# A decoder layer with two linear-attention mixers: two chunks in one matmul in the delta rule's inverse, with a wider step table

## The chip, the cores and the metric

The kernel runs on one core of one Trainium2 chip. The metric is the device time of one execution in microseconds (us). Three runs of the kernel before gave 2825.11, 2827.06 and 2832.34 us; the median is 2827.06.

## The reference

One layer of a decoder: 2048 tokens of width 1024, float32. An input projection feeds four heads of a gated delta rule and four heads of HGRN2 (128 wide each); then come an output projection, an MLP of 4096 with squared ReLU, and a gated embedding. The part that the change touches is the delta rule, in chunks of c tokens:

```python
lmat = jnp.einsum('bhncd,bhnsd->bhncs', k_beta, k) * decay
a_mat = jnp.eye(c) + jnp.where(strict, lmat, 0.0)
u = solve(v_beta)                                  # a_mat u = v_beta
w = solve(k_beta * jnp.exp(gc)[..., None])
...
def step(s, inp):
    v_new = u_n - w_n @ s
    o = qg_n @ s + qk_n @ v_new
    s = s * cd_n[..., None, None] + kt_n.T @ v_new
    return s, o
```

So each chunk needs the inverse of a unit triangular matrix, and the chunks of one head follow each other through the state `s`. The kernel uses chunks of 128 tokens.

## The kernel before

Everything is one function, `trunk`, for one core. Tokens are cut into four quarters (`q`) of 512 (`QT`), each into four chunks (`NC`) of 128. The first half of the execution is the mixer stage, the second the output projection, MLP and gate, which the change leaves alone.

**The mixer stage.** A list of projections (`works`) is gone through in order: per quarter one small one for the decays (`ab`) and eight for each of four heads (k, q, v, z of the delta rule, then f, i, q, g of HGRN2). Each is 24 matmuls of 128x512 on split float32 operands. After every eight of them `tick()` is called: this text calls what happens there a *turn*. A projection has three turns, a head 24. In a turn, Python generators that stand in an agenda take their next step; between two `yield`s lies one step. `gdn_mixer` (delta rule) and `hgrn_mixer` are such generators, with one step for each entry of the tables `A_STEPS` and `B_STEPS`, counted in turns from the head's start; the last head has tables of its own, `A_LAST` and `B_LAST`. A step at 34 is thus taken at turn 10 of the next head, beside that head's own steps; in one turn the older head comes first, and in a head the delta rule ahead of HGRN2. TensorE's order and that of SP's DMA queue are the program's; the other engines' order is the scheduler's.

**The delta rule's steps.** The convolution (`conv_silu`) leaves k, q, v as tiles of 128x512 (`kT`, `qT`, `vT`) with Silu as one ACT instruction. Then, by step (in turns of the head):

- 3 and 6: the decays are loaded and spread (`gf`), the masked exponentials `e` are made from the mask `negm`.
- 7 to 9: k is turned on TensorE (bank `psk`); its squared norm gives `rk`, `cc`, `ncc`, `inv` (through a power on POOL).
- 10: eight matmuls into two banks (`kk`), from which DVE makes the chunk's triangular matrix `u` and the scores `qk`, and multiplies `kT` and `qT` by `gf`.
- 12: v is turned; the 32x32 diagonal blocks of `u` are stored to memory (`ud`, four DMAs).
- 14 to 22: the blocks come back spread over the partitions (`sys`), and DVE inverts them all by a triangular solve of 16 passes (L621 to L626).
- 24 and 26: the inverses go out (`xd`) and come back as block diagonals into `xx`, which POOL cleared (one 128x512 memset, four DMAs).
- 28: DVE transposes them (four instructions, L641).
- 30 to 36: two levels (`lev` 5 and 6) fill in the blocks off the diagonal: 4 matmuls `psp` (L651), a copy `half`, then 8 or 4 matmuls `psd` (L657, L658) and copies back into `xx` (L662, L663). All have 64 columns, one matmul for each chunk and side.
- 38 to 49: the recurrence over the four chunks, three steps each: `psa` (kg and the state, then DVE makes `r`, L671), `psb` (the inverse and `r`, then ACT makes `w`, L676), `psc` (then DVE makes the new state, L681) with two matmuls into `pso`. One turn lies between two steps.
- 50 to 59: `finish` squares, sums over the partitions (`nrm`, L261), stores the row (L266), loads it as `m` (L269), takes a power on POOL, stores that (L274), loads it spread (L236), scales and stores (L530).

Banks: `pp` has four, for nearly all of these; `po` has two, for `pso`; `pm` two, for the projections. `kT` and `qT` have two buffers, `ktail`, `vt` and `qk` two, `xx`, `um` and `half` one.

Of the kernel before, what the change touches and what calls it, by code (L numbers as in the profile page):

```python
# [20 lines left out]
P = 128  # L21
# [20 lines left out]

C_IDENT, C_NEG, C_UNIT, C_MASK = 0, 1, 2, 3
N_CONST = C_MASK + len(LEVELS)
# [17 lines left out]
def constants():  # L62
    j = np.arange(P)[:, None]
    i = np.arange(P)[None, :]
    c = np.zeros((P, N_CONST, P), np.float32)
    c[:, C_IDENT] = (i == j)
    c[:, C_NEG] = np.where(j <= i, 0.0, -1e30)
    c[:, C_UNIT] = (i % SB == GC * (j % GR) + i // SB)
# [11 lines left out]
def trunk(ctx, tc, x, xT, pT, vecs, w_in, w_ab, gdn_a_log, gdn_dt_bias, w_out, w_up, w_down,  # L80
# [19 lines left out]
    def blk(c):  # L100
        return slice(c * P, (c + 1) * P)
# [6 lines left out]
    ident = cst[:, C_IDENT, :]  # L108
    negm = cst[:, C_NEG, :]
# [3 lines left out]
    def over_chunks(m):  # L113
        return m[:, None, :].broadcast_to([P, NC, P])

# [281 lines left out]
    with mixers as mctx:  # L397
# [11 lines left out]
        V.memset(bound, 0.0)  # L409
        um = {lev: mp.tile([P, NC, P], F32, name=f"um{lev}") for lev in (5, 6)}  # L410
        half = mp.tile([P, NC, P], F32, name="half")
        for t in (*um.values(), half):
            V.memset(t, 0.0)
# [40 lines left out]
        def decays(ps, q):  # L454
# [18 lines left out]
            nc.sync.dma_start(gd, gb[0:4, :])  # L473
            yield
            ps = bank(f"ps_gb_{q}", ph)
            for c in range(NC):
                PE.transpose(ps[:, c * 36 : (c + 1) * 36], gb[:, blk(c)], ident[:36, :36])
            gcol = sm.tile([P, NC, 36], F32, tag="gcol", name=f"gcol_{q}", bufs=2)
# [12 lines left out]

        def conv_silu(ps, j, name, tag, bufs):

# [7 lines left out]
            y = m2.tile([P, QT], F32, tag=tag, name=f"y_{name}", bufs=bufs)  # L501
            call(clock[0], lambda: S.activation(y, acc, AF.Silu))
            return y

        def turned(src, name, pool=None):
# [10 lines left out]
        def finish(q, h, pso, zt, extra, eps, n):  # L516
# [13 lines left out]
            nc.sync.dma_start(mixd[q][h], og)  # L530

        def gdn_mixer(q, h, live):

# [14 lines left out]
            e = mt(f"e_{n}", "e")  # L548
            V.tensor_tensor(e, gf, over_chunks(negm), ALU.add)
            for c in range(NC):  # L550
# [32 lines left out]
            for c in range(0, NC, 2):  # L583
                ps = bank(f"kk_{n}_{c}", pp).rearrange("p (a b i) -> p a b i", a=2, b=2)
                for a in range(2):
                    sl = blk(c + a)
                    PE.matmul(ps[:, a, 0, :], kT[:, sl], kT[:, sl], start=True, stop=True)
                    PE.matmul(ps[:, a, 1, :], kT[:, sl], qT[:, sl], start=True, stop=True)
                for a in range(2):
                    V.scalar_tensor_tensor(u[:, c + a, :], ps[:, a, 0, :], ncc[:, c + a : c + a + 1],  # L590
                                           e[:, c + a, :], ALU.mult, ALU.mult)
                V.tensor_tensor(qk[:, c : c + 2, :], ps[:, :, 1, :], e[:, c : c + 2, :], ALU.mult)
            V.tensor_tensor(kT, kT, flat(gf), ALU.mult)
            V.tensor_tensor(qT, qT, flat(gf), ALU.mult)
# [10 lines left out]
            yield  # L605
            for lev in (5, 6):
                s = LEVELS[lev]
                for o in range(0, P, 2 * s):
                    S.activation(um[lev][o : o + s, :, o + s : o + 2 * s], u[o : o + s, :, o + s : o + 2 * s], AF.Copy)
            sys = mt(f"sys_{n}", "sys", 1, (P, SB, SB))  # L610
# [22 lines left out]

            xx = mt(f"xx_{n}", "xx", 1, (P, NC, 2 * P))
            G.memset(xx[:, :, P:], 0.0)
            for b in range(NB):
                nc.sync.dma_start(xx[b * SB : (b + 1) * SB, :, P + b * SB : P + (b + 1) * SB],
                                  xd[:, b].rearrange("c j i -> j c i"))
            yield
            for c in range(NC):  # L640
                V.transpose(xx[:, c, :P], xx[:, c, P:])  # L641
            for lev in (5, 6):
                s = LEVELS[lev]
                yield

                psp = bank(f"psp_{n}_{lev}", pp)[:, : QT // 2].rearrange("p (c b s) -> p c b s", c=NC, s=s)
                left = xx[:, :, :P].rearrange("p c (b two s) -> p c b two s", two=2, s=s)[:, :, :, 0]
                right = xx[:, :, P:].rearrange("p c (b two s) -> p c b two s", two=2, s=s)[:, :, :, 1]
                part = half.rearrange("p c (b two s) -> p c b two s", two=2, s=s)[:, :, :, 0]
                for c in range(NC):  # L650
                    PE.matmul(psp[:, c], um[lev][:, c, :], left[:, c], start=True, stop=True)  # L651
                S.activation(part, psp, AF.Copy)
                yield
                psd = bank(f"psd_{n}_{lev}", pp).rearrange("p (c two b s) -> p c two b s", c=NC, two=2, s=s)
                for c in range(NC):
                    if lev == 5:
                        PE.matmul(psd[:, c, 0], xx[:, c, P:], part[:, c], start=True, stop=True)  # L657
                    PE.matmul(psd[:, c, 1], half[:, c, :], right[:, c], start=True, stop=True)  # L658
                for i in range(P // (2 * s)):
                    o = 2 * s * i  # L660
                    if lev == 5:
                        S.activation(left[o + s : o + 2 * s, :, i], psd[o + s : o + 2 * s, :, 0, i], AF.Copy)  # L662
                    S.activation(right[o : o + s, :, i], psd[o : o + s, :, 1, i], AF.Copy)  # L663
            yield
            pso = bank(f"pso_{n}", po)
            for c in range(NC):
# [6 lines left out]
                psb = bank(f"psb_{n}_{c}", pp)[:, :P]  # L673
                PE.matmul(psb, xx[:, c, P:], r, start=True, stop=True)
                w = m2.tile([P, P], F32, tag="w", name=f"w_{n}_{c}")
# [117 lines left out]
        def to_k(ps, q, h, g, b):  # L793
            g["k"] = conv_silu(ps, 4 + h, f"kg{q}_{h}", "kT", 2)

        def to_q(ps, q, h, g, b):
            g["q"] = conv_silu(ps, h, f"qg{q}_{h}", "qT", 2)

        def to_v(ps, q, h, g, b):
            g["v"] = conv_silu(ps, 8 + h, f"vg{q}_{h}", "vT", 1)  # L800

# [873 lines left out]
```

## Time and profile before

| | us |
|---|---|
| median of three runs | 2827.06 |
| lowest, highest | 2825.11, 2832.34 |
| the profiled execution | 2829.28 |
| its span in the profile | 2827.5 |
| TensorE (PE) busy | 2736.0 |
| VectorE (DVE) busy | 2041.8 |
| ScalarE (ACT) busy | 1448.3 |
| TensorE's granted clock | 0.991 of full |

The profile lists instructions by engine, line and tile. In a group's row stand its form (partitions x elements), its count, then the busy time and the mean in ns of one, then the idle time of the engine just before and what ended it. PE is TensorE's matmuls, PEld its weight loads, SPq the DMA queue of SyncE. An f32 matmul of the mixers appears as two instructions. In the views of waits a row says who waited for whom: us in total, times, longest. A busy TensorE may still be slower than it could be, since a matmul's end is modelled and the next one starts before it.

### The profile page before, as it was taken

Reading aid. Unit: us, or ns where it says so; the run is one execution under the profiler, and the core shown is the slowest. Engines: PE = TensorE matmul, PEld = TensorE weight load, DVE = VectorE, ACT = ScalarE, POOL = GpSimd, SP = SyncE. Lnnn points to the kernel's source line nnn. Section 1 sums busy time; section 2 is a strip of 40 time slices with the busy share of each in tenths; the row PEclk is TensorE's granted clock in tenths of the full one; section 3 lists DMA queues with packets and bytes.
Section 4 is the critical chain, followed back from the end, with each engine's and each line's share of the span. In section 5 each row is a group of like instructions: output and inputs, shape, how many; then the busy total and the mean of one; then the engine's idle time right before and its main releaser. Section 6 shows DMA issues by size and latency. Waiting matters only on the chain.

```text
span 2827.5 us, 38753 instructions
## 1 busy us (share of the span) xinstructions
PE 2736.0 (97%) x13041; PEld 2258.5 (80%) x13041; DVE 2041.8 (72%) x4236; ACT 1448.3 (51%) x2761; POOL 110.3 (4%) x104
## 2 busy tenths in 40 slices
PE   7999999999999999898999999999999999999999
PEld 5788788888888888786778887888888888887887
DVE  6677767786777777667797876767787765567775
ACT  6565545454545444565555555555555445455431
POOL 0000000000000000000000000000100000001000
PEclk9999999999999999999999999999999999999999
DMA  7766667656656665686575547666454446577663
GB/s 246 262 219 214 210 228 256 208 199 227 226 198 210 219 210 174 201 294 228 176 241 191 199 145 241 209 212 242 152 199 159 148 148 218 190 253 243 206 217 116
DMA packets 268598, 589.19 MB, mean 208 GB/s; under 512 B 55642, under 2 KB 59960, under 8 KB 249200
## 3 DMA queue, kind: packets, MB, share of 16 engines
q1 hardware_dynamic: 268400, 586.72, 61.9%
q8 instruction: 103, 1.69, 0.2%
q14 instruction: 95, 0.78, 0.1%
HBM read 419.68 MB, written 166.92 MB: 207 GB/s over the span
## 4 chain that ended last, share of the span: by engine, by line
PE 48%; DMA 4%; DVE 3%; ACT 2%; issue 2%; SPq 0%; POOL 0%; DVEq 0%; ACTq 0%; POOLq 0%
PE u L1031 21%; PE d L1031 18%; PE mmg L1031 6%; PE mmo L1031 2%; DMA raw_out<-in_w_out_dram 1%; DMA da<-sumd 1%; DMA db<-hid 1%; DMA b<-h1d 0%; DVE w_out L162 0%; DMA mixT<-mixd 0%; DVE t L162 0%; ACT w_out L161 0%; ACT L1068 0%; DVE b L1178 0%; PE mmo L991 0%
## 5 line engine op out<-in xcount | busy, mean ns | idle before, releaser
L963 PE MATMUL mm<-xt,w 128*128 128x512 f32 x3072 | 781.2, 402 | 4.9 <-DVE acc_vg L499 4.5
L963 PEld LDWEIGHTS mm<-xt,w 128*128 128x128 f32 x3072 | 562.3, 190 | 117.9 <-issue 3.4
L1031 PE MATMUL d<-db,da 128*128 128x512 f32 x2688 | 612.6, 389 | 4.0 <-DVE db L215 3.5
L1031 PE MATMUL u<-t,wu 128*128 128x512 f32 x2604 | 608.0, 396 | 3.4 <-ACT wu L161 3.3
L1031 PEld LDWEIGHTS d<-db,da 128*128 128x128 f32 x2688 | 504.1, 188 | 111.8 <-DVE db L215 5.7
L1031 PEld LDWEIGHTS u<-t,wu 128*128 128x128 f32 x2604 | 489.5, 188 | 121.2 <-ACT wu L161 4.1
L215 DVE TENSOR_TENSOR db<-db 128x512 fp32r<-128x512 f32 x224 | 161.5, 721 | 73.9 <-ACT db L214 73.5
L1360 DVE TENSOR_TENSOR u<-u,u 128x512 f32<-128x512 f32 x224 | 150.3, 682 | 74.4 <-PE u L1031 74.1
L1031 PE MATMUL mmo<-mixT,w_out 128*128 128x512 f32 x720 | 171.7, 399 | 11.4 <-DVE w_out L162 7.8
L214 ACT ACTIVATE db<-db 128x512 fp32r<-128x512 f32 x224 | 140.8, 629 | 81.0 <-DMA db<-hid 80.0
L1031 PE MATMUL mmg<-h2T,wg 128*128 128x512 f32 x768 | 178.1, 394 | 0.0
L1401 ACT ACTIVATE u<-u 128x512 f32<-128x512 f32 x128 | 80.9, 632 | 181.4 <-DVE u L1360 181.0
L1031 PEld LDWEIGHTS mmo<-mixT,w_out 128*128 128x128 f32 x720 | 136.8, 191 | 45.3 <-DVE w_out L162 9.1
L1031 PEld LDWEIGHTS mmg<-h2T,wg 128*128 128x128 f32 x768 | 144.3, 188 | 33.5
L162 DVE TENSOR_TENSOR da<-da 128x512 fp32r<-128x512 f32 x128 | 92.9, 726 | 89.4 <-ACT da L161 89.1
L161 ACT ACTIVATE da<-da 128x512 fp32r<-128x512 f32 x128 | 80.5, 629 | 137.3 <-DMA da<-sumd 120.2
L621 DVE TENSOR_TENSOR pr_g<-xs_g,sys_g 128x16 f32<-128x16 f32 (+14 forms) x240 | 94.2, 392 | 5.1
L161 ACT ACTIVATE wu<-a 128x512 fp32r<-128x512 f32 x124 | 74.1, 624 | 46.1 <-DMA a<-in_w_up_dram 43.9
L225 POOL TENSOR_TENSOR acc_y<-acc_y,sq_y 128x512 f32<-128x512 f32 x28 | 38.7, 1384 | 1396.6 <-ACT sq_y L224 1396.6
L162 DVE TENSOR_TENSOR wu<-a,wu 128x512 fp32r<-128x512 f32 x124 | 84.7, 686 | 3.8 <-ACT wu L161 3.8
L1402 ACT ACTIVATE u<-u 128x512 f32<-128x512 f32 x128 | 80.8, 631 | 3.7
L162 DVE TENSOR_TENSOR da<-dr,da 128x512 fp32r<-128x512 f32 x96 | 66.2, 689 | 16.5 <-ACT da L161 14.4
(362 smaller groups left out, 3892.3 us busy)
## 6 DMA issues: line engine op xcount, KB each, us to landing
w<-cache_in SPq DMA_DIRECT2D x96, 1024.0 KB
db<-hid SPq DMA_DIRECT2D x224, 256.0 KB
cache_in<-w SPq DMA_DIRECT2D x32, 1024.0 KB
hid<-u SPq DMA_DIRECT2D x128, 256.0 KB
da<-sumd SPq DMA_DIRECT2D x128, 256.0 KB
a<-in_w_up_dram SPq DMA_DIRECT2D x124, 256.0 KB
hid<-ht SPq DMA_DIRECT2D x96, 256.0 KB
dr<-in_w_down_dram SPq DMA_DIRECT2D x96, 256.0 KB
```

Source lines behind the costliest of these rows:

```text
L161: S.activation(t[:, 0], raw, AF.Copy)
L162: eng.tensor_tensor(t[:, 1], raw, t[:, 0], ALU.subtract)
L214: S.activation(t[:, 0], plain(t), AF.Copy)
L215: V.tensor_tensor(t[:, 1], plain(t), t[:, 0], ALU.subtract)
L225: eng.tensor_tensor(acc, acc, sq, ALU.add)
L621: V.tensor_tensor(pr[:, :, :, 0:i], xs[:, None, :, 0:i].broadcast_to([P, 2, GC, i]), sys[:, 0:i, i : i + 2].rearrange("p j two -> p two j" ...
L963: PE.matmul(ps, *terms[i], start=i == 0, stop=i == nt - 1)
L1031: PE.matmul(ps, a, b, start=start, stop=stop)
L1360: V.tensor_tensor(c[new], c[old], ps, ALU.add)
L1401: S.activation(c[k], c[k], AF.Relu)
L1402: S.activation(c[k], c[k], AF.Square)
```

## The change

*Two chunks in one matmul.* The four 32-blocks of every odd chunk are kept in reverse order, so that its triangular matrix has its blocks on the other side of the diagonal; an even and an odd chunk then fill one 128x128 matrix. The reversal is made where the data arise: Silu of k and v is written in two halves, the odd one with blocks backwards; the decays are transposed from a reversed copy (`back`); a second mask plane is added; `u` of odd chunks is made with `e` read backwards; `kT` is multiplied by `gf` in two halves. q stays as it is. The inverse works on pairs: `xt` (block diagonals of both chunks of a pair), `xn` (its transpose, one DVE instruction), `um` and `part` by pair, ten matmuls of 128 columns instead of twenty of 64, and a last set of copies into `xt_full`, from which `psb` reads.

*The step table.* The steps from 30 on move: psp5 to 32, the inverse to 32 to 38, the recurrence to 40 to 55 with two turns between `psa` and `psb`, `finish` to 56 to 65. `A_LAST` is given the same values as before from its sixteenth entry on.

*Buffers.* `kT` and `qT` get three.

```diff
-A_STEPS = ((3, 6, 7, 8, 9, 10, 12, 14, 16, 17, 18, 19, 20, 21, 22, 24, 26, 28, 30, 32, 34, 36)
-           + tuple(range(38, 50)) + (50, 52, 54, 55, 57, 59))
+A_STEPS = ((3, 6, 7, 8, 9, 10, 12, 14, 16, 17, 18, 19, 20, 21, 22, 24, 26, 28, 32, 34, 36, 38)
+           + (40, 42, 43, 44, 46, 47, 48, 50, 51, 52, 54, 55)
+           + (56, 58, 60, 61, 63, 65))
...
-            call(clock[0], lambda: S.activation(y, acc, AF.Silu))
+            def last():
+                if back:
+                    S.activation(even(y), even(acc), AF.Silu)
+                    S.activation(odd(y), odd_back(acc), AF.Silu)
+                else:
+                    S.activation(y, acc, AF.Silu)
+            call(clock[0], last)
...
-            V.tensor_tensor(kT, kT, flat(gf), ALU.mult)
+            V.tensor_tensor(even(kT), even(kT), even(flat(gf)), ALU.mult)
+            V.tensor_tensor(odd(kT), odd(kT), odd_back(flat(gf)), ALU.mult)
...
-            for lev in (5, 6):
-                s = LEVELS[lev]
-                for o in range(0, P, 2 * s):
-                    S.activation(um[lev][o : o + s, :, o + s : o + 2 * s], u[o : o + s, :, o + s : o + 2 * s], AF.Copy)
+            up = by_pair(u)
+            for g in range(NB):
+                S.activation(um[5][rows_of(g), :, rows_of(g ^ 1)], up[rows_of(g), :, g % 2, rows_of(g ^ 1)], AF.Copy)
+            for a in range(2):
+                S.activation(um[6][halves[a], :, halves[1 - a]], up[halves[a], :, a, halves[1 - a]], AF.Copy)
...
-            xx = mt(f"xx_{n}", "xx", 1, (P, NC, 2 * P))
-            G.memset(xx[:, :, P:], 0.0)
...
-            for c in range(NC):
-                V.transpose(xx[:, c, :P], xx[:, c, P:])
...
+            xt = mt(f"xt_{n}", "xt", 1, (P, NC, P // 2))
+            xn = mt(f"xn_{n}", "xn", 1, (P, NC, P // 2))
+            G.memset(xt, 0.0)
+            for g in range(NB):
+                nc.sync.dma_start(xt[rows_of(g), :, rows_of(g % 2)], xd[:, g].rearrange("c j i -> j c i"))
+            yield
+            V.transpose(flat(xn), flat(xt))
+            yield
+            def pairs(out, lhsT, rhs):
+                for p in range(2):
+                    PE.matmul(out[:, p], lhsT[:, p], rhs[:, p], start=True, stop=True)
...
+            psp = pair_bank("psp5")
+            pairs(psp, um[5], two(xn))
+            for g in range(NB):
+                S.activation(part[5][rows_of(g), :, rows_of(g ^ 1)], psp[rows_of(g), :, rows_of(0 if g % 2 else 3)],
+                             AF.Copy)
+            yield
+            psx, pst = pair_bank("psx5"), pair_bank("pst5")
+            pairs(psx, two(xt), part[5])
+            pairs(pst, part[5], two(xt))
+            for g, to in ((1, 0), (2, 1)):
+                V.tensor_copy(by_pair(xn)[rows_of(g), :, g // 2, rows_of(to)], psx[rows_of(g), :, rows_of(3 * to)])
+            for g in range(NB):
+                at_b = rows_of(1 + g % 2)
+                S.activation(two(xt)[rows_of(g), :, at_b], pst[rows_of(g), :, at_b], AF.Copy)
+            yield
+            psp = pair_bank("psp6")
+            pairs(psp, um[6], two(xn))
+            for a in range(2):
+                S.activation(part[6][halves[1 - a], :, halves[a]], psp[halves[1 - a], :, halves[a]], AF.Copy)
+            yield
+            psd = pair_bank("psd6")
+            pairs(psd, part[6], two(xt))
+            xf = by_pair(xt_full)
+            for a in range(2):
+                S.activation(xt_full[halves[a], :, halves[a]], xt[halves[a]], AF.Copy)
+            for a in range(2):
+                S.activation(xf[halves[a], :, a, halves[1 - a]], psd[halves[a], :, halves[a]], AF.Copy)
...
-                PE.matmul(psb, xx[:, c, P:], r, start=True, stop=True)
+                PE.matmul(psb, xt_full[:, c, :], r, start=True, stop=True)
...
-            g["k"] = conv_silu(ps, 4 + h, f"kg{q}_{h}", "kT", 2)
+            g["k"] = conv_silu(ps, 4 + h, f"kg{q}_{h}", "kT", 3, True)
...
-            g["q"] = conv_silu(ps, h, f"qg{q}_{h}", "qT", 2)
+            g["q"] = conv_silu(ps, h, f"qg{q}_{h}", "qT", 3, False)
```

More of the change, by code (lines that the diff above doesn't have):

```diff
@@ L409, in trunk @@
         V.memset(bound, 0.0)
-        um = {lev: mp.tile([P, NC, P], F32, name=f"um{lev}") for lev in (5, 6)}
-        half = mp.tile([P, NC, P], F32, name="half")
-        for t in (*um.values(), half):
+        um = {lev: mp.tile([P, NC // 2, P], F32, name=f"um{lev}") for lev in (5, 6)}
+        part = {lev: mp.tile([P, NC // 2, P], F32, name=f"part{lev}") for lev in (5, 6)}
+        xt_full = mp.tile([P, NC, P], F32, name="xt_full")
+        for t in (*um.values(), *part.values(), xt_full):
             V.memset(t, 0.0)
```

63 lines of the change are left out of this document (29 added, 34 removed).

## The prediction, made before the changed kernel was built or run

> **What bounds the kernel now.** I read the busy shares first, then the mixer stage alone, then who makes TensorE wait there.
>
> ```profile
> span 2827.5 us, 38753 instructions
> PE 2736.0 (97%) x13041; PEld 2258.5 (80%) x13041; DVE 2041.8 (72%) x4236; ACT 1448.3 (51%) x2761; POOL 110.3 (4%) x104
> ```
>
> ```profile
> 174.20:1066.60 892.40, 866.19 (x4794) 738.29 (x4792) 653.16 (x1891) 435.01 (x1024) 52.30 (x54) 0.99 0.65 215
> ...
> 1132.30:1207.50 75.20, 64.21 (x334) 53.88 (x333) 47.31 (x100) 43.55 (x85) 6.14 (x6) 0.95 0.62 205
> ```
>
> The second fence gives stretches of the span: length, then busy PE, PEld, DVE, ACT, POOL, clock, DMA share, GB/s. The first is thirteen heads, 2 to 14, together 321 turns (a turn is what follows each eight projection matmuls): 2.78 us a turn, 66.7 us a head of 24. TensorE is busy for 866 of 892 us, DVE for 73%, ACT for 49%. So a matmul taken out of the mixers is worth its own time, as long as nothing new is waited for. The second stretch is the last head's tail, with 11 us of idle TensorE.
>
> ```profile
> PE psb_g L674 <- DVE r_g L671: 14.9, 21, 2.8
> PE psp_g L651 <- ACT xx_g L662: 7.5, 5, 2.8
> PE psp_g L651 <- DVE xx_g L641: 5.2, 4, 2.4
> ...
> PE psa_g L669 <- DVE S_g L681: 2.7, 2, 1.4
> ```
>
> These are TensorE's waits in the mixers (us, times, longest). The big one is psb, which needs r from DVE one turn after psa. Then the inverse: its second product waits for ACT's copies, its first for DVE's transposes.
>
> **Fewer matmuls.** The inverse has 20 f32 matmuls of 64 columns a head; afterwards it has 10 of 128 columns (psp5, psx5, pst5, psp6, psd6, two each). Each appears as two instructions.
>
> ```profile
> L651 PE MATMUL psp_g<-xx_g,um 128*128 128x64 f32 x256 | 33.9, 276 | 12.7 <-ACT xx_g L662 7.5 <-DVE xx_g L641 5.2
> L657 PE MATMUL psd_g<-half,xx_g 128*128 128x64 f32 x128 | 23.8, 268 | 0.0
> L658 PE MATMUL psd_g<-xx_g,half 128*128 128x64 f32 x256 | 41.8, 277 | 1.6 <-ACT half L652 1.6
> ```
>
> ```profile
> 546.53 0.33 PE L657 MATMUL psd_g<-half,xx_g 128*128 128x64 f32 x2
> ...
> 548.26 0.66 PE L758 MATMUL at_h<-qk_h,keys_h 128*128 128x128 f32 x4
> ```
>
> ```profile
> 554.36 0.39 PE L587 MATMUL kk_g<-y_kg 128*128 128x128 f32 x2
> ...
> 556.06 4.07 PE L963 MATMUL mm<-xt,w 128*128 128x512 f32 x16
> ```
>
> The first gives 256 + 128 + 256 = 640 instructions, 40 a head. In the timeline sixteen of 64 columns run from 546.53 to 548.26, 1.73 us or 0.108 each; sixteen of 128 columns (kk) run from 554.36 to 556.06, 1.70 us or 0.106 each. So width costs nothing here, and the count alone pays: 640 x 0.108 - 320 x 0.106 = 69.1 - 33.9 = 35 us off. Bounds: 0 if a merged matmul took twice as long, 36 at most; I take 35, since kk has the very shape.
>
> [...]
>
> **Other engines' work for it.** ACT's copies, DVE's transposes and two neighbours by which to price the new ones:
>
> ```profile
> L609 ACT ACTIVATE um<-u_g 32x128 f32<-32x128 f32 (+1 forms) x48 | 16.4, 342 | 7.7 <-DVE u_g L590 7.1
> L652 ACT ACTIVATE half<-psp_g 128x256 f32<-128x256 f32 x32 | 12.2, 381 | 20.9 <-PE psp_g L651 20.8
> L662 ACT ACTIVATE xx_g<-psd_g 32x128 f32<-32x128 f32 x32 | 8.6, 269 | 5.1 <-PE psd_g L658 4.7
> L763 ACT ACTIVATE keys_h<-qk_h 128x256 f32<-128x256 f32 x80 | 33.2, 415 | 35.2 <-DVE qk_h L760 33.3 <-PE at_h L758 0.6 <-PE ps_gb L477 0.4
> L502 ACT ACTIVATE y_kg<-acc_kg 128x512 f32<-128x512 f32 x16 | 10.0, 624 | 17.0 <-DVE acc_kg L500 17.0
> L593 DVE TENSOR_TENSOR y_kg<-y_kg,gf_g 128x512 f32<-128x512 f32 x16 | 10.9, 680 | 0.0
> L641 DVE STREAM_TRANSPOSE xx_g<-xx_g 128x128 f32<-128x128 f32 x64 | 14.7, 278 | 0.0
> ```
>
> Before, ACT does 3 um, 2 half and 5 xx copies a head, about 3 x 0.34 + 2 x 0.38 + 5 x 0.27 = 3.1 us. After: 6 um, 4 + 2 part, 4 into xt, 4 into xt_full, twenty in all, each between 0.27 and 0.42, mostly of 64 elements: about 20 x 0.29 = 5.8. Silu of k and v goes in two halves, 2 x (2 x 0.42 - 0.62) = 0.4. So ACT gains 3 us a head on 32.5: no bound by itself, but it matters where ACT is full (below). DVE loses four transposes (1.1) for one of 256 columns (between 0.28 and 0.56), gets two small copies from psx (0.2 to 0.28 each), and splits one multiply of 0.68 into two halves (0.34 to 0.42 each): within 0.3 us a head of nothing. The 64 KB of constants more are loaded under the embedding; the third kT and qT buffers cost memory only, and cover that a two-buffer kT would be rewritten 48 turns on, at turn 51, while the recurrence now reads it until 55 instead of 49.
>
> **The moved steps.** psp5 follows the transposes by four turns instead of two: its 5.2 us of waiting for DVE goes. psb follows psa by two turns instead of one: the 14.9 go, but for the last head, whose own step table isn't changed and which has the 2.8: 12 off. What is late next is S: psc to the following psa stays one turn.
>
> ```profile
> 524.71 0.38 PE L669 MATMUL psa_g<-S_g,y_kg 128*128 128x128 f32 x2
> ...
> 526.78 0.48 PE L674 MATMUL psb_g<-r_g,xx_g 128*128 128x128 f32 x2
> ```
>
> ```profile
> 526.38 0.34 DVE L671 SCALAR_TENSOR_TENSOR r_g<-vt_g,inv_g,psa_g 128x128 f32<-128x128 f32 x1
> ```
>
> ```profile
> sum 70.70, PE 69.79 PEld 59.48 DVE 66.96 ACT 17.06 POOL 1.14; mean PE 13.96 PEld 11.89 DVE 13.39 ACT 3.41 POOL 0.23
> ```
>
> The last row sums turns 19 to 23 of five heads (70.7 us): DVE is busy for 95%, with the triangular solve. There r, due right after psa ends at 525.1, starts at 526.4, and psb starts late. With the new table the second psc falls on turn 23 and the third psa on the next, the same place: S meets the same queue. It has the two pso matmuls, 0.45 us, more time than r had, but these turns become about 1 us shorter for TensorE. So part of psb's wait comes back at psa. Bounds 0 and 20 us; I take 7, half of what goes.
>
> **ACT at turns 7 to 10.** This is where the second product of the inverse waits for ACT.
>
> ```profile
> sum 67.50, PE 66.23 PEld 58.69 DVE 35.13 ACT 58.66 POOL 10.08; mean PE 13.25 PEld 11.74 DVE 7.03 ACT 11.73 POOL 2.02
> ```
>
> ```profile
> L264 ACT ACTIVATE osq_g<-nrm_g 1x512 f32<-1x512 f32 x16 | 9.3, 581 | 14.6 <-PE nrm_g L262 14.5
> L520 ACT ACTIVATE osq_g<-pso_g 128x512 f32<-128x512 f32 x16 | 9.5, 596 | 21.5 <-PE pso_g L683 21.5
> L161 ACT ACTIVATE hl_g<-osq_g 128x512 fp32r<-128x512 f32 x16 | 10.0, 626 | 7.4 <-DVE osq_g L523 7.4
> ```
>
> Turns 7 to 10 of five heads: ACT busy 58.7 of 67.5 us, 87%. The later finish of the head before puts its square and split (0.60 + 0.63) into turn 8 and its row copy (0.58) into turn 10, and the four copies into xt come there too (1.1 for 0.38): about 2.5 us more a head, in a time that gets 1 us shorter. The copies to part[5] at turn 8 are what psx5 at turn 10 needs; behind ACT's exponentials and squares they come as late as the xx copies do now, 7.5 us in 5 heads. I add 6 (bounds 0 and 25). Where they are late, kk, hgrn's level and the projection stand behind psx5 on TensorE. Turn 10 also asks for six banks of a pool of four (norm, psx, pst, hgrn's level, two kk): kk's second waits until DVE has copied psx. I take 2 (0 to 10).
>
> **SP's queue.** Each finish step issues its DMA at the new place: norm's store, load and store at turns 10, 12, 13 of the next head, then rsb's load and mixd's store at 15 and 17. They were at 4, 6, 7, 9, 11. So the store of m, which waits for POOL, now stands ahead of the load of sys, with which the solve starts.
>
> ```profile
> 541.11 0.32 SPq L269 DMA_DIRECT2D m_g<-sd_g  x1
> 548.09 0.32 SPq L274 DMA_DIRECT2D rd_g<-m_g  x1
> ...
> 559.41 2.31 SPq L604 DMA_DIRECT2D ud_g<-u_g  x4
> 564.55 0.53 SPq L611 DMA_DIRECT2D sys_g<-ud_g  x1
> ```
>
> ```profile
> SPq L274 <- POOL m_g L157: 130.0, 16, 13.2
> ```
>
> ```profile
> DVE xs_g L626 <- DMA sys_g<-ud_g: 18.8, 12, 2.9
> ```
>
> From m's load to its store SP takes 7 us here, waiting 8.1 a head on average. If the load of m goes just ahead of ud's stores, its store follows 7 to 8 us on, where sys could go 5.1 us after ud (559.41 to 564.55): sys is 0 to 3 us late. DVE already waits for sys in twelve heads, so the solve begins later and weighs on turns 19 to 23, while the weights behind it on SP are two projections ahead. I take 4 us in all (0 to 40). The last head takes more copies in the same one-turn steps: 1 us (-2 to 4).
>
> **Sum.** -35 - 5 - 12 + 7 + 6 + 2 + 4 + 1 = -32. The profiled execution took 2829.28 us (span 2827.5), 2.2 above the median of 2827.06; from its own time the sum gives 2797, against the median 2795. I say 2796.
>
> **Rivals.**
> (a) All waits dissolve: wider steps also cover psx5, S and the banks. Then -35 - 5 - 12 - 7 = -59 (ACT's 7.5 too): 2769. For it: 26 us of idle in 892 is all there is; against: DVE at 95% where S falls.
> (b) The waits change place and take nearly everything: S 18, ACT 20, banks 4, sys 7, last head 1: -52 + 50 = -2: 2826. For it: DVE at 95% and ACT at 87% in the turns that get more or less time.
> (c) Slower, by SP alone: m's store holds sys. L270's turn on DVE now lies among the u, qk and kT work, and the store can take the 13.2 seen, against 5.1 that ud's flight hides: 8 us. DVE's free time from turn 14 on covers some 3 of them; beyond that point each us delays S and psa. 5 us in 15 heads is 75: -52 + 7 + 6 + 2 + 75 + 1 = +39, and half of it, 2.5 a head, gives +1; in between, 2847.
> (d) The change doesn't do what it says: a 128-column matmul costs twice a 64-column one, and 35 falls away: -32 + 35 = +3, 2830. The kk row speaks against it. [...]
>
> **Chances.** Forecast 0.57 (own range 2782 to 2812), (a) 0.15, (b) 0.12, (c) 0.13, (d) 0.03. Below about 0.3%, 8.5 us, this kernel's runs don't tell a difference from none. Faster: 0.57 + 0.15 + a quarter of (b), less a little at the edge, 0.74; same: the rest of (b), (d) and some of (c), 0.13; slower: 0.13. The range 2768 to 2828 takes in (a), (b) and the unknown costs of one sign, and leaves out (c) and the tails.
>
> **What would show it.** 320 matmul records for the inverse at about 0.106 us each; no psp wait on the transpose; psb's waits nearly gone outside the last head; new waits of psa for S around turn 0, of psx for ACT's part copies; the store of m ahead of sys, and how long DVE waits for sys. I am wrong if the merged matmuls are spaced 0.2 us, if DVE's wait for sys grows several times, or if the psx wait passes 25 us.

## The result and the profile after

| | median us | ratio to before | 95% interval |
|---|---|---|---|
| before (four runs beside it) | 2829.70 | | |
| changed | 2856.61 | 1.0096 | 1.0073 to 1.0119 |

Slower by 27 us, where 32 less was forecast. The first fence is the mixer stage before, without the last head's tail, the second the same after: stretch and length, then busy PE, PEld, DVE, ACT, POOL, granted clock, DMA share, GB/s.

```profile
51.60:1132.30 1080.70, 1045.51 (x5727) 888.56 (x5727) 789.74 (x2273) 537.73 (x1256) 62.96 (x64) 0.99 0.65 216
```

```profile
51.40:1158.50 1107.10, 1028.34 (x5410) 864.52 (x5409) 790.73 (x2273) 570.12 (x1441) 56.00 (x64) 0.98 0.64 211
```

All of the loss is in this stage, 26.4 us. TensorE is busy there for 17.2 us less and idle for 78.8 us in place of 35.2. So some 33 us of matmuls did go (e5 below shows the figure undisturbed), but 44 us of idle time came. Busy time fell by less than what was taken out, since the clock was lower: by the clock records of the two traces TensorE ran at half rate for 20.5 us of the stage before and for 51.2 after, which is 15 us more of busy time. 44 + 15 - 33 gives the 26. The groups of the inverse's matmuls, and then TensorE's waits in the mixers, show both:

```profile
L679 PE MATMUL psp_g<-xn_g,um 128*128 128x128 f32 x128 | 19.4, 274 | 0.0
...
L679 PE MATMUL psx_g<-part,xt_g 128*128 128x128 f32 x64 | 13.3, 344 | 7.1 <-POOL rk_g L156 7.1
```

```profile
PE nrm_g L260 <- ACT hl_g L160: 25.0, 8, 5.6
PE psa_g L721 <- DVE S_g L733: 14.4, 24, 1.9
PE pso_h L838 <- DVE S_h L837: 12.8, 20, 1.7
PE psx_g L679 <- POOL rk_g L156: 7.1, 3, 3.6
PE nrm_g L261 <- DVE hl_g L161: 5.6, 10, 1.0
```

With 64 each of pst and psd that is 320 instructions, half of 640. The same form takes 274 ns in psp, but 344 in psx, which stands at turn 10 behind the waits. The transposes' wait is gone and psb's too. What came instead is a wait nobody priced: the norm of the older head, 25 + 5.6 us, with single standstills of 5 us. One of them, at turn 10 of the eighth head: first ACT and DVE, then TensorE.

```profile
564.50 0.63 ACT L544 ACTIVATE osq_g<-pso_g 128x512 f32<-128x512 f32 x1
...
567.51 0.63 ACT L160 ACTIVATE hl_g<-osq_g 128x512 fp32r<-128x512 f32 x1 [0.59 <-DVE osq_g L547]
```

```profile
566.79 0.68 DVE L547 TENSOR_TENSOR osq_g<-osq_g,q_g 128x512 f32<-128x512 f32 x1
...
568.17 0.69 DVE L161 TENSOR_TENSOR hl_g<-osq_g,hl_g 128x512 fp32r<-128x512 f32 x1
```

```profile
568.19 0.80 PE L260 MATMUL nrm_g<-hl_g,ones 128*128 128x512 f32 x1 [5.12 <-ACT hl_g L160]
...
569.51 1.05 PE L679 MATMUL psx_g<-part,xt_g 128*128 128x128 f32 x4
```

The square waits on ACT until the next head's exponentials and the squares of its k are through (564.5); the sum with `q2` is made on DVE at 566.8, the split on ACT at 567.5, its second half on DVE at 568.2. These are four crossings between two full engines, and psx, kk and the projection (which starts at 574.5) stand in TensorE's queue behind the norm. After the standstill the norm's matmul takes 0.80 us, and four psx instructions 1.05.

### The profile page after: what moved, and what is told of

Same layout as the page of the kernel before. It is cut to its first block, busy times and chain, and to the rows that moved or that the text cites. A ratio compares the mean times of both kernels' runs of the same rounds, so it can differ in the third digit from the quotient of the medians.

```text
span 2852.0 us, 38340 instructions
## 1 busy us (share of the span) xinstructions
PE 2720.2 (95%) x12721; PEld 2232.7 (78%) x12721; DVE 2044.6 (72%) x4242; ACT 1482.6 (52%) x2955; POOL 103.1 (4%) x104
## 4 chain that ended last, share of the span: by engine, by line
PE 47%; DVE 4%; DMA 3%; ACT 2%; issue 2%; POOL 0%; SPq 0%; DVEq 0%; ACTq 0%; POOLq 0%
PE u L1083 21%; PE d L1083 17%; PE mmg L1083 6%; PE mmo L1083 1%; DMA da<-sumd 1%; DMA raw_out<-in_w_out_dram 1%; DMA xo<-in_xT_dram 0%; DMA b<-h1d 0%; DVE t L161 0%; ACT da L160 0%; DVE w_out L161 0%; ACT L1120 0%; PE mme L187 0%; DVE b L1230 0%; DVE db L214 0%
## 5 line engine op out<-in xcount | busy, mean ns | idle before, releaser
L660 DVE SCALAR_TENSOR_TENSOR xs_g<-xs_g,sys_g 128x4 f32<-128x4 f32 x256 | 57.7, 225 | 43.6 <-DMA sys_g<-ud_g 38.1
```

The source lines that it names most:

```text
L660: V.scalar_tensor_tensor(xs[:, :, i + 1], xs[:, :, i], sys[:, i, i + 1 : i + 2], xs[:, :, i + 1], ALU.mult, ALU.add)
```

## The experiments

Each run stood beside runs of the kernel before on its own chip, so ratios compare; 0.001 is 2.8 us. The diffs show the entries of the table from the inverse on.

| run | median us | ratio | 95% interval |
|---|---|---|---|
| e1_old_steps | 2817.32 | 0.9952 | 0.9936 to 0.9969 |
| e2_finish_only | 2843.98 | 1.0040 | 1.0021 to 1.0059 |
| e3_norm_one_later | 2858.50 | 1.0096 | 1.0077 to 1.0115 |
| e5_close | 2802.15 | 0.9895 | 0.9870 to 0.9920 |
| e6_close_late_finish | 2833.93 | 1.0005 | 0.9993 to 1.0017 |
| e7_scale_later | 2857.92 | 1.0088 | 1.0071 to 1.0105 |
| e8_split_on_dve | 2863.90 | 1.0112 | 1.0095 to 1.0128 |
| e9_wide_old_inverse | 2831.79 | 1.0002 | 0.9991 to 1.0013 |
| e10_close_dma_past_sys | 2828.17 | 1.0022 | 1.0013 to 1.0032 |
| e11_finish_past | 2847.72 | 1.0095 | 1.0080 to 1.0111 |
| e12_close_copies_on_dve | 2802.16 | 0.9925 | 0.9904 to 0.9946 |
| e13_after_copies_on_dve | 2846.76 | 1.0094 | 1.0077 to 1.0111 |
| e14_close_late | 2843.36 | 1.0042 | 1.0030 to 1.0054 |
| e15_fill | 2861.64 | 1.0104 | 1.0086 to 1.0121 |
| e16_norm_early | 2829.18 | 0.9985 | 0.9974 to 0.9997 |
| e17_before_later | 2828.13 | 0.9987 | 0.9974 to 1.0000 |
| e18_fill_long | 2857.37 | 1.0083 | 1.0067 to 1.0100 |
| e19_only_scaling_late | 2800.44 | 0.9886 | 0.9871 to 0.9901 |

**The parts alone.** In the changed kernel the old table (e1), and in the kernel before the late finish only (e2):

```diff
-A_STEPS = ((3, 6, 7, 8, 9, 10, 12, 14, 16, 17, 18, 19, 20, 21, 22, 24, 26, 28, 32, 34, 36, 38)
-           + (40, 42, 43, 44, 46, 47, 48, 50, 51, 52, 54, 55)
-           + (56, 58, 60, 61, 63, 65))
+A_STEPS = ((3, 6, 7, 8, 9, 10, 12, 14, 16, 17, 18, 19, 20, 21, 22, 24, 26, 28, 30, 32, 34, 36)
+           + tuple(range(38, 50)) + (50, 52, 54, 55, 57, 59))
```

```diff
-           + tuple(range(38, 50)) + (50, 52, 54, 55, 57, 59))
+           + tuple(range(38, 50)) + (56, 58, 60, 61, 63, 65))
```

> The changed kernel with the step table of before (inverse at 30 to 36, recurrence at 38 to 49, finish at 50 to 59); the paired inverse and the third buffers stay. Theory F (finish's place: its square, split and norm now fall on turns 8 to 10, where ACT is full, and norm's matmul stands first in TensorE's queue at turn 10): the 30 us of norm waits go, the 35 us of merged matmuls stay; psb waits come back (15): 2790 to 2805, 25 to 40 below before. Rival C (copies: the paired inverse's twenty ACT copies make ACT late whatever finish does): 2825 to 2850, with psx or psd waits over 25 us.

> The kernel before with finish alone at 56, 58, 60, 61, 63, 65; inverse and recurrence as before. Theory F: norm waits of 25 to 35 us appear at turn 10 and the time rises by 20 to 40, to 2850 to 2870. Rival C, and rival R (the recurrence with two turns between psa and psb puts S on turns 19 and 23, where DVE is late, and costs the time): no norm wait to speak of, 2825 to 2835.

Neither run came out as either of its theories had it. The merged matmuls by themselves gain 0.5%, 14 us: from the turning of v in the first head to that in the last, TensorE is busy for 958 us instead of 986, but idle for 50 instead of 31. The late finish by itself loses 0.4%, 11 us, and no norm waits there (1.4 us in all); psb does, for 26.2 us in place of 14.9. So the changed kernel's loss is in the moved steps: from e1 to it they cost 0.0144, 41 us.

**Single waits of the changed kernel.** The norm one turn later (e3), the last two steps past the solve (e7), the norm's split on DVE (e8):

```diff
-           + (56, 58, 60, 61, 63, 65))
+           + (56, 59, 61, 62, 64, 66))
```

```diff
-           + (56, 58, 60, 61, 63, 65))
+           + (56, 58, 60, 61, 73, 75))
```

```diff
-        split(hl, V, acc)
+        if name[0] == "g":
+            V.tensor_copy(hl[:, 0], acc)
+            V.tensor_tensor(hl[:, 1], acc, hl[:, 0], ALU.subtract)
+        else:
+            split(hl, V, acc)
```

> The changed kernel with finish at 56, 59, 61, 62, 64, 66 (one head, the last but one, as in the changed kernel): the square and split stay at turn 8, norm's matmul goes from turn 10 to 11, behind psx, hgrn's level and kk. Theory F: norm's wait falls from 31 us to under 8 and 20 to 30 us go: 2825 to 2838. Rival C: psx then waits in norm's place for ACT's part copies, 20 us or more, and the time stays at 2850 to 2860.

> The changed kernel with the last two steps of finish (load of rsb with DVE's scaling, and mixd's store) at 73 and 75 in place of 63 and 65, so at turns 1 and 3 and not 15 and 17; the last head but one as it was. Theory D (at turn 15 DVE waits for rsb in front of the solve, and is late for S at turns 19 and 20): psa's and pso_h's waits for S fall from 27 us to under 14 and 10 to 20 us go: 2837 to 2847. If DVE is late there only because sys comes late and the turns are shorter: S waits stay above 22, 2850 to 2860.

> The changed kernel with the delta rule's norm split wholly on DVE (its copy of 128x512 goes from ACT to DVE). Theory F in its narrow form (ACT's split at turn 8 is what holds norm's matmul): norm waits fall from 31 us to under 8, and 15 to 30 us go: 2827 to 2842. Rival C (ACT is the bound of turns 7 to 10 and the next matmul that needs it waits instead): psx waits take the place with 15 us or more, 2850 to 2860.

None gains. In e7 psa's and pso's waits for S stay at 26 us together; in e3 the norm's wait moves on to others, and in e8 it stays. TensorE's largest waits of e3, then of e8:

```profile
PE pso_h L839 <- DVE S_h L838: 27.0, 18, 5.8
PE psx_g L680 <- POOL rk_g L157: 20.4, 8, 6.1
```

```profile
PE nrm_g L264 <- DVE hl_g L258: 29.1, 9, 6.0
```

**Close and wide.** e5 keeps the merged matmuls and the later inverse, with the recurrence at one step a turn and the finish right behind it; e6 is e5 with the changed kernel's finish; e9 has the wide recurrence two turns earlier, behind the old places of the inverse. Each line replaces the recurrence's and the finish's entries:

```diff
-           + (40, 42, 43, 44, 46, 47, 48, 50, 51, 52, 54, 55)
-           + (56, 58, 60, 61, 63, 65))
+           + tuple(range(40, 52))
+           + (52, 54, 56, 57, 59, 61))
```

```diff
-           + (40, 42, 43, 44, 46, 47, 48, 50, 51, 52, 54, 55)
+           + tuple(range(40, 52))
```

```diff
-           28, 32, 34, 36, 38)
-           + (40, 42, 43, 44, 46, 47, 48, 50, 51, 52, 54, 55)
-           + (56, 58, 60, 61, 63, 65))
+           28, 30, 32, 34, 36)
+           + (38, 40, 41, 42, 44, 45, 46, 48, 49, 50, 52, 53)
+           + (54, 56, 58, 59, 61, 63))
```

> The changed kernel with the inverse at 32 to 38 as changed, but the recurrence at 40 to 51, one turn between all steps, and finish at 52, 54, 56, 57, 59, 61, so that norm's matmul is at turn 6. Theory F: norm's wait goes, psb waits of 10 to 20 us come back: 2795 to 2815. Rival C: 2840 to 2860. Rival R: psa and pso_h waits for S fall from 27 us to under 8, and that is the larger part of the gain.

> The paired inverse at 32 to 38 and the close recurrence at 40 to 51 as in the run with the close recurrence (2802), but finish at the changed kernel's 56, 58, 60, 61, 63, 65. Theory F (finish's place): norm waits of 15 us or more at turn 10, and 25 to 45 us more than 2802: 2827 to 2847. Rival R (two turns between psa and psb): no norm wait, 2798 to 2812.

> The changed kernel with the inverse at the old 30 to 36, the recurrence with two turns between psa and psb at 38 to 53, and finish at 54, 56, 58, 59, 61, 63: norm's matmul at turn 8. It differs from the run with the old table (2817) by the wide recurrence and a finish four turns later. Rival R: S waits of 20 us or more, 2835 to 2860. Theory F: turn 8 comes before ACT's backlog is worst, norm waits under 10 us: 2805 to 2825.

e5 beats both kernels. Its mixer stage, columns as above:

```profile
52.60:1101.10 1048.50, 1012.42 (x5418) 856.02 (x5417) 795.96 (x2279) 567.38 (x1438) 57.81 (x64) 0.99 0.68 222
```

TensorE is idle for 36.1 us, as before the change, and its busy time is 33.1 lower: here the merged matmuls are cashed in whole. From e5 to e6 four turns' delay of the finish cost 0.011, 31 us, though the norm waits for 1.4 us only. (The same delay cost 11 us in e2: what a place costs depends on the other places.) In e6 it is psb and psx that wait:

```profile
PE psb_g L726 <- DVE r_g L723: 16.4, 21, 3.2
PE psx_g L679 <- issue: 11.4, 7, 2.9
```

e9 fits neither of its theories whole: psa and pso wait 26 us for S and the norm 6, at 1.0002. The same steps two turns on are the changed kernel, and cost 0.009 more.

**Which part of the late finish.** e16 is e5 with only the last four finish steps late, e19 with only the last two, e10 is e6 with the last four later still, to go behind the system's transfers (the last head but one keeps its steps), e14 is e6 with the close recurrence four turns later:

```diff
-           + (52, 54, 56, 57, 59, 61))
+           + (52, 54, 60, 61, 63, 65))
```

```diff
-           + (52, 54, 56, 57, 59, 61))
+           + (52, 54, 56, 57, 63, 65))
```

```diff
-           + (56, 58, 60, 61, 63, 65))
+           + (56, 58, 64, 65, 67, 69))
```

```diff
-           + tuple(range(40, 52))
+           + tuple(range(44, 56))
```

> The close recurrence (2802 us) with the finish's square, split and norm left at steps 52 and 54 and only its mean, its scaling and its store as late as in the run with the late finish (60, 61, 63, 65; 2834 us). If the place of the square, split and norm in turns 8 to 10 costs the 32 us: 2798 to 2812 us. If the mean's wait, the scaling on VectorE and the store at turns 12 to 17 cost them: 2822 to 2838 us.

> The close recurrence with all of the finish early (52, 54, 56, 57) but its scaling and store, which stand at 63 and 65 as in the late finish. If the mean's load and store on SyncE, ahead of the system's transfers, cost the 26 us that the run with norm early kept: 2798 to 2810 us, the solve's first pass back near 13 us behind turn 12. If the scaling on VectorE at turn 15, ahead of the solve's passes, costs them: 2820 to 2834 us, the first pass near 15 us.

> The close recurrence with the late finish (2834 us) with the mean's load and store moved from steps 60 and 61 to 64 and 65, and the last two steps to 67 and 69: SyncE then issues the system's transfers for the next solve ahead of the finish's own. Only the head before the last keeps the old steps. Theory Q (SyncE's order: the finish's transfers stand ahead of the system's, and the solve starts some 2 us late): 2812 us or less, the solve's first pass back near 13 us behind turn 12, the waits of TensorE for psb back to about 7 us. Theory P (what costs is the place of the finish's square, split and sums on ScalarE and VectorE in turns 8 to 10, which are full): 2828 to 2840 us, the waits for psx and psb as they were.

> The changed kernel with the recurrence close (one step a turn) but late, at steps 44 to 55, so that it ends where the wide one ends; the finish at 56 to 65 as in the changed kernel. Theory L (the recurrence's end at step 55 is what costs: the finish's square and split then fall into turns 8 to 10 and the norm waits): 2845 to 2862 us, TensorE's waits for the norm's split 18 us or more. Theory W (the two turns between psa and psb cost): 2825 to 2840 us, like the close recurrence with the late finish (2834), waits for the norm's split under 6 us.

e16 keeps nearly all of the cost, e19 has none of it: 0.010, 28 us, hang on the place of the mean's two steps alone. The sixth head shows it at its strongest. First e16, the DMA issues of SP, then rows of DVE and of TensorE; then e19, SP and TensorE:

```profile
419.50 0.32 SPq L273 DMA_DIRECT2D rd_g<-m_g  x1
...
421.36 2.80 SPq L636 DMA_DIRECT2D ud_g<-u_g  x4
...
429.29 0.53 SPq L645 DMA_DIRECT2D sys_g<-ud_g  x1
```

```profile
415.64 0.16 DVE L269 TENSOR_SCALAR m_g<-m_g 128x4 f32<-128x4 f32 x1
...
427.99 0.75 DVE L552 SCALAR_TENSOR_TENSOR og_g<-og_g,cols,rsb_g 128x512 f32<-128x512 f32 x1 [4.69 <-DMA rsb_g<-rd_g]
...
430.22 0.34 DVE L723 SCALAR_TENSOR_TENSOR r_g<-vt_g,inv_g,psa_g 128x128 f32<-128x128 f32 x1
433.84 0.23 DVE L660 SCALAR_TENSOR_TENSOR xs_g<-xs_g,sys_g 128x4 f32<-128x4 f32 x1 [3.27 <-DMA sys_g<-ud_g]
```

```profile
417.32 0.60 PE L532 MATMUL t_vg<-cst,y_vg 128*128 128x128 f32 x4
...
430.71 0.76 PE L726 MATMUL psb_g<-r_g,xt_full 128*128 128x128 f32 x2 [2.04 <-DVE r_g L723]
431.12 3.45 PE L1015 MATMUL mm<-xt,w 128*128 128x512 f32 x8
434.41 0.38 PE L731 MATMUL psc_g<-w_g,kt_g 128*128 128x128 f32 x2
```

```profile
411.67 2.69 SPq L636 DMA_DIRECT2D ud_g<-u_g  x4
...
419.74 0.53 SPq L645 DMA_DIRECT2D sys_g<-ud_g  x1
```

```profile
413.31 0.60 PE L532 MATMUL t_vg<-cst,y_vg 128*128 128x128 f32 x4
...
424.65 2.10 PE L1015 MATMUL mm<-xt,w 128*128 128x512 f32 x8
426.58 0.38 PE L731 MATMUL psc_g<-w_g,kt_g 128*128 128x128 f32 x2
```

Measured from the turning of v at turn 12 (417.32 and 413.31), the four stores of `ud` start at +4.0 in e16 and at -1.6 in e19, the load of `sys` at +12.0 and +6.4. m's load was issued at 405.14, but its turn on DVE (L269) comes only at 415.64, among the next head's u, qk and kT, and POOL's power behind that. So m's store goes out only at +2.2; SP stood there for 10.4 us, and the load of rsb, which needs that store, and ud's stores stand behind it in SP's queue.

Two waits of DVE follow. It stands 4.69 us for rsb, with which the finish scales; r, made behind that, is late, and psb waits 2.04 us for it. Then it stands 3.27 us for `sys`, and the solve's first pass comes at +16.5 for +11.1 in e19 (424.42): of the 5.5 us by which the load is late, 5.4 reach the solve. The eight projection matmuls behind psb take 3.45 us for 2.10, and psc comes at +17.1 for +13.3.

The sixth head is not the common case. The head that finishes started 48 turns before the one whose solve is next, but 51 where a quarter's small projection (`ab`, three turns) comes between. In six of the fourteen heads 3 to 16 (5, 6, 9, 10, 13, 14) m's load and store therefore stand at turns 9 and 10, ahead of ud's. In the other eight they stand at 12 and 13, and only `sys` is right behind m's store, as in the eighth head (m's store at 558.33, `sys` at 558.85). There psb waits behind the solve's first passes:

```profile
565.26 0.23 DVE L660 SCALAR_TENSOR_TENSOR xs_g<-xs_g,sys_g 128x4 f32<-128x4 f32 x1 [4.56 <-DMA sys_g<-ud_g]
```

```profile
566.83 0.46 PE L726 MATMUL psb_g<-r_g,xt_full 128*128 128x128 f32 x2 [2.70 <-DVE xs_g L658]
```

On the average of the fourteen heads the load of `sys` is 2.3 us later than in e19 and the solve's first pass 2.8 us (12.5 for 9.7 us behind turn 12). TensorE's waits in the stage for r, for the passes ahead of r and for S are 25.0 us in place of 7.5. DVE's waits in the whole stage, e16 and then e19:

```profile
DVE xs_g L660 <- DMA sys_g<-ud_g: 35.9, 14, 4.6
...
DVE og_g L552 <- DMA rsb_g<-rd_g: 16.8, 5, 5.4
```

```profile
DVE xs_g L660 <- DMA sys_g<-ud_g: 7.5, 6, 2.5
...
DVE og_g L552 <- DMA rsb_g<-rd_g: 6.4, 4, 2.8
```

e10 is no faster than e6 (1.0022 against 1.0005), but tests the queue only in part. In the same six heads its steps 64 and 65 fall on turns 13 and 14, so that m's load and store are again ahead of `sys`; the first pass comes 14.9 us behind turn 12 there (14.8 in e6). In the other eight the mean is behind `sys`, and the first pass comes at 8.4 us in place of 11.1. That these eight earlier solves show in no gain speaks against the load of `sys` as the whole of the 28 us; the new places may cost what it gives. How the 28 us divide between DVE's two waits stays open.

```profile
DVE xs_g L661 <- DMA sys_g<-ud_g: 30.0, 8, 5.2
```

e14 came between its two theories: the late end of the recurrence costs 0.004 over e6, 10 us, and the two turns between psa and psb the rest, 0.005, up to the changed kernel. Its waits, where the norm's for ACT is a third of the changed kernel's:

```profile
PE pso_h L838 <- DVE S_h L837: 22.8, 9, 4.9
...
PE nrm_g L260 <- ACT hl_g L160: 8.4, 4, 3.4
```

**The finish later still; the small copies on DVE.** e11 puts the whole finish behind turn 10 in the changed kernel (`q2` in bfloat16, three buffers; the last head but one keeps its steps); e12 (in e5) and e13 (in the changed kernel) take eight small copies off ACT:

```diff
-           + (56, 58, 60, 61, 63, 65))
+           + (59, 62, 64, 65, 67, 69))
...
-            q2 = m2.tile([P, QT], F32, tag="q2", name=f"q2_{n}")
+            q2 = m2.tile([P, QT], BF16, tag="q2", name=f"q2_{n}", bufs=3)
```

```diff
-                S.activation(part[5][rows_of(g), :, rows_of(g ^ 1)], psp[rows_of(g), :, rows_of(0 if g % 2 else 3)],
-                             AF.Copy)
+                V.tensor_copy(part[5][rows_of(g), :, rows_of(g ^ 1)], psp[rows_of(g), :, rows_of(0 if g % 2 else 3)])
...
-                S.activation(two(xt)[rows_of(g), :, at_b], pst[rows_of(g), :, at_b], AF.Copy)
+                V.tensor_copy(two(xt)[rows_of(g), :, at_b], pst[rows_of(g), :, at_b])
```

> The changed kernel with the whole finish later still, steps 59, 62, 64, 65, 67, 69, so that its square and split come after turns 8 to 10 where ScalarE is full; the finish's last copy of the output is held in bfloat16 and three buffers to make room, and the head before the last keeps its steps. Theory F (the loss is the norm's matmul standing in TensorE's queue at turn 10 behind a full ScalarE): TensorE's waits for the norm's split fall from 25 us to under 5, turn 10 falls from 9.5 to about 6 us, and the time to 2820 to 2838 us. Theory R (the two turns between the recurrence's parts and its lateness): 2850 to 2860 us, the waits on S (14 us and 13 us) stay.

> The close recurrence (2802 us) with the eight small copies of the paired inverse (the last part and the transposes) on VectorE in place of ScalarE. Theory C (ScalarE is the bound of turns 7 to 10, and its copies hold psx): the waits of TensorE for psx (5 us and 5 us) go, and the time is 2785 to 2798 us. Rival: VectorE, which also has the splits of the inverse there, is as late: 2800 to 2812 us.

> The changed kernel with the same eight copies on VectorE. Theory C (ScalarE's copies of the paired inverse are what makes the norm's split late in turn 10): the wait for the split falls from 25 us to under 12, and the time to 2838 to 2848 us. Theory F (the finish's own square and split are late, since the output is complete only in turn 7): 2850 to 2865 us, with the wait for the split at 20 us or more.

None gains, by the ratios: 1.0095 and 1.0094 against the changed kernel's 1.0096, and 0.9925 against e5's 0.9895. (The medians of e11 and e13 look lower only because the kernel before ran 2821 us beside them.) In e11 the norm's wait is gone and the time is not: S is late instead, at psa for 25.0 us, and psx waits for 11.7 us:

```profile
PE psa_g L722 <- DVE S_g L734: 25.0, 18, 3.6
PE psx_g L680 <- POOL rk_g L157: 11.7, 3, 4.9
```

With the copies on DVE the norm still waits 24.6 us for ACT's split (e13), so ACT's new copies are not what makes it late.

**Is the lower clock the loss?** e15 and e18 put 12 and 23 matmuls that nothing reads ahead of the three norms with the longest standstills:

```diff
         ps = bank(f"nrm_{name}", pool or pp)
+        if name in ("g0_0", "g0_1", "g1_1"):
+            for _ in range(23):
+                PE.matmul(ps.rearrange("p (a b) -> p a b", b=P), ones, ones[:, None, :].broadcast_to([P, NC, P]),
+                          start=True, stop=True)
         PE.matmul(ps, ones, hl[:, 0, :], start=True, stop=False)
```

> The changed kernel with twelve 128x512 matmuls of ones, which nothing reads, ahead of the norm of three heads of sixteen: those where TensorE stood still for 5.6, 5.6 and 5.1 us ahead of it. They take some 12 x 0.40 = 4.8 us each of time that was idle. Theory K (each long standstill costs a second time, by the granted clock behind it): granted clock 1.00 in the three places, some 2.5 to 4 us less at each, 2845 to 2851 us. Rival: only the standstill counts, and the matmuls cost nothing or delay the norm: 2856 to 2862 us.

> The changed kernel with 23 matmuls of ones, which nothing reads, ahead of the same three norms: at 0.227 us each some 5.2 us, nearly the whole of the standstills of 5.6, 5.6 and 5.1 us. Theory K (the granted clock falls behind a standstill and costs a second time): the clock stays at 0.95 or more in the 20 us behind each of the three, 2.5 to 4 us are won at each, and the time is 2843 to 2851 us where the changed kernel has 2857. Rival: the clock there falls all the same, or the three gains are lost in later waits: 2854 to 2862 us.

The twelve took only 2.9 us of each standstill. The 23 fill it; the changed kernel and then e18, in 20 us around each:

```profile
200.00:220.00 20.00, 13.38 (x71) 11.38 (x70) 12.51 (x32) 16.61 (x50) 1.01 (x1) 0.83 0.43 154
280.00:300.00 20.00, 16.67 (x83) 14.80 (x83) 13.13 (x36) 12.62 (x31) 1.02 (x3) 0.74 0.29 86
560.00:580.00 20.00, 14.88 (x74) 12.81 (x73) 11.41 (x36) 15.25 (x49) 1.01 (x1) 0.83 0.38 139
```

```profile
200.00:220.00 20.00, 18.32 (x90) 15.43 (x89) 12.03 (x32) 16.59 (x48) 1.01 (x1) 0.91 0.49 168
280.00:300.00 20.00, 18.31 (x97) 15.70 (x96) 13.25 (x37) 13.69 (x37) 2.18 (x3) 0.91 0.30 90
560.00:580.00 20.00, 17.42 (x95) 14.46 (x94) 11.41 (x35) 15.51 (x49) 1.01 (x1) 1.00 0.38 139
```

The clock is better in all three, and no gain is seen: 1.0083 lies inside the changed kernel's interval. The intervals alone would leave room for the 7.5 us that theory K asks at least, so the three heads themselves: from the turning of v in the head before to their own, the changed kernel takes 71.9, 76.8 and 72.6 us, e18 72.3, 74.5 and 74.2. One wins 2.3 us, two lose 2.0. The third shows where it went:

```profile
572.55 0.46 PE L620 MATMUL kk_g<-y_kg 128*128 128x128 f32 x2 [1.37 <-DVE xn_g L703]
```

The norm's matmul takes 0.50 us now for 0.80, and kk waits 1.37 us for the bank that DVE's copies from psx hold; the projection starts at 574.42, where it started at 574.51. So in this stretch the other engines' chain sets the length, and TensorE's slow clock was hidden under it. In the two others the low clock came later, from pst or from the matmul behind it on.

**The place without the merge.** e17 gives the kernel before the steps of e5:

```diff
-           28, 30, 32, 34, 36)
-           + tuple(range(38, 50)) + (50, 52, 54, 55, 57, 59))
+           28, 32, 34, 36, 38)
+           + tuple(range(40, 52)) + (52, 54, 56, 57, 59, 61))
```

> The kernel before, one chunk in a matmul, two buffers, with only its inverse's last three steps, its recurrence and its finish two turns later (inverse to 38, recurrence 40 to 51, finish from 52: the steps of the 2802 us run). If the later place gains by itself, as it did beside the merged matmuls (2802 against 2817): 2808 to 2820 us. If the place gains only where the merged matmuls have freed TensorE: 2824 to 2838 us.

By itself the later place gains at most 0.003; with the merged matmuls it gained 0.006 (e5 against e1).

## Why the prediction was wrong

**Fewer matmuls, -35: right.** 33 us of busy time went (e5), and width cost nothing, so rival (d) fell. But that it all reaches the time was not right as such: with the old steps only 14 us did (e1).

**The waits that go, -5 and -12: right.** In the changed kernel psp waits for nothing and psb for 2.1 us. **New waits of psa for S, +7:** 14.4 in the row, where 2.7 were before: 12, inside its bounds; the same lateness at pso for HGRN2's state, 12.8, wasn't priced.

**SP's queue, +4: one step that failed.** It was named with its mechanism (m's store ahead of `sys`) and bounded at 40; alone, in the close kernel, the mean's place costs 28 us (e16 against e19). I let ud's flight and DVE's free time cover nearly all of it, and nothing was covered: the solve's first pass is as late as the load. The term also left out DVE's stand for rsb, and counted all heads as 48 turns apart, while in six of them m's store is ahead of ud's stores too. This was rival (c)'s mechanism, at 0.13 too low, though (c) put all on `sys`. In the changed kernel it wasn't tried alone with the norm left late. What its trace shows is that DVE's wait for `sys` doubled, from 18.8, and that the solve's first pass comes 12.0 us behind turn 12 for 10.9 before: an estimate from that is 16 us in fourteen heads, if every late us counts.

```profile
DVE xs_g L660 <- DMA sys_g<-ud_g: 38.1, 14, 3.8
```

**ACT at turns 7 to 10, +6: the other step that failed.** It counted ACT's added work (2.5 us a head) and looked for who waits at psx, with 25 us at most. The norm's matmul, which stands ahead of psx in TensorE's queue, had no price, and waits for 30.6 us. The finish's square needs the whole output, which the recurrence now completes in turn 7, and the chain through ACT and DVE is late as a chain, whichever engine has the split (e8) or the copies (e13). The late output isn't all of it: e14 completes it in the same turn, and its norm waits for 12.9 us. Why the two turns between psa and psb add 18 to that stays open. e6 to e14 to the changed kernel is 0.009, 26 us, for the late and the wide recurrence together. **Banks, +2:** hidden under that chain; it came out in e18, where kk waited.

**The signs.** None of the three that were to show the forecast wrong came: the merged matmuls aren't spaced 0.2 us, the wait for `sys` doubled only, and psx waits for 7.1 us. The wait that grew stood one place ahead of the one that was watched.

**The sum.** One way from run to run, in ratios to the kernel before: 0.9886 with scaling late only; + 0.010 for the mean's place; + 0.002 for square, split and norm late (e6 against e16), hardly more than the noise; + 0.004 for the late end (e14); + 0.005 for the width: 1.0096. Another way gives other shares, since the places act on each other (e2). That the first of these kernels stands at the forecast's -32 is chance: it hasn't the moves. In the forecast's own terms, the merge was -35 and the moves -17 + 20 = +3; measured are -14 for the merge (e1) and +41 for the moves behind it.

## What to carry to other kernels

A step that is moved takes its DMAs with it: look up what the new neighbours in an in-order queue start, and take a store that waits for a slow engine as a wall for all that stands behind it. Move it ahead of the chain that starts there or leave it, count the turns for every head and not for the common one, and don't count on the flight of a transfer that is itself behind the wall. Widening one wait away in a ring of steps makes the last step of the ring late: here 17 us of waits at psb and the transposes went, and 31 came at the norm, where the ring's output is used. So change the work (the merge) and the places in separate runs, and keep the places that were good.

## What the runs showed of the hardware

A standstill of TensorE can cost a second time, by the granted clock behind it. In the changed kernel one of 2.84 us, ahead of psx at turn 10 of the sixth head, was followed by 10 us at a granted clock of 0.83, four psx instructions taking 1.19 us, where four of that form took 0.66 in the prediction's timeline:

```profile
430.00:440.00 10.00, 9.67 (x55) 9.03 (x56) 9.06 (x27) 7.55 (x24) 1.14 (x2) 0.83 0.29 58
```

```profile
430.33 1.19 PE L679 MATMUL psx_g<-part,xt_g 128*128 128x128 f32 x4 [2.84 <-POOL rk_g L156]
```

The Trainium skill's page TensorE: Matmul & The Clock Gate, part "The HAM clock gate", has the clock halved after an idle window of some 3.4 us and full again after a busy one. A loss of 0.17 of 10 us is about one such window at half rate, an estimate from that page that fits the row; but here 2.84 us of standing still were enough. The trace's clock record has one stretch of 3.4 us at half rate there, from 430.2 us on. Whether the second cost counts is another matter: in the sixth head of e16, at a clock of 0.62 from 431 to 435 us, it made eight matmuls behind psb 1.35 us longer; at turn 10 of the three filled heads (e18) taking it away won nothing.
